# Feed-forward input with the tokens as rows: h2 stationary, 512 weight columns moving, products turned back

## The chip, the cores and the metric

The kernel runs on one NeuronCore of a Trainium2 chip. The metric is the device time of one execution in microseconds, as the median of several runs. All times below are of that core.

## The reference

One layer of a hybrid diffusion backbone (256 latent tokens, 256 context tokens, width 2048, float32): an adaLN-modulated mixer (multi-head latent attention and bidirectional HGRN2, merged by gates), then an adaLN-modulated SwiGLU feed-forward. Cut to what matters here:

```python
D_MODEL, SEQ, CTX_LEN = 2048, 256, 256
D_FF = 5632                      # 44 blocks of 128

def mixer_projections(h, w_in_l, ...):
    p = h @ w_in_l               # for the latent and for the context stream
    c_q, c_kv, k_r, hg_q, hg_ff, hg_fb, hg_i, hg_g, gate_logits = jnp.split(p, ...)
    ...
    hq = heads(jax.nn.silu(hg_q)) * (HG_FDIM ** -0.5)

def swiglu(h, w_in_l, w_out_l):
    a, b = jnp.split(h @ w_in_l, 2, axis=-1)
    return (jax.nn.silu(a) * b) @ w_out_l

# in reference(), last layer (the only one):
x = x + gt_a * rmsnorm(out_l, norm_g[layer, 1])
h = modulate(rmsnorm(x, norm_g[layer, 2]), sh_f, sc_f)          # h2 below
x = x + gt_f * rmsnorm(swiglu(h, w_ffn_in[layer], w_ffn_out[layer]), norm_g[layer, 3])
```

Of the context stream, only what the latent one needs is computed (keys, values, HGRN2 states). c_q, hg_q, hg_g and the gates are needed for the latent stream alone: these are the single-stream blocks.

## The kernel before

Every large product is made of three: a float32 value is split into a high part H (rounded to fp32r by ScalarE, a CAST) and a low part L (the difference, by VectorE), and weight times activation is H·H + H·L + L·H, added up in PSUM. Weights come as tiles `raw` of 128 x 2048 (1 MB) on SP's queue through three buffers (`load_w`), and are split in halves of 1024 columns into `wH` and `wL`, which have three buffers each (`split_w`). Activations live split in the tile `hx`, two parts side by side.

There are two ways to lay a product out.

- Weights stationary: a 128x128 block of the weight stands in TensorE and the 256 tokens move. `mm3` issues three matmuls (H with aH, H with aL, L with aH), of 256 columns for one stream or 512 for two. `mm_wide` has one stream's aH and aL side by side and issues H with both (512 columns) and L with aH (256); the two halves of the PSUM bank are then added by a ScalarE copy and a VectorE addition. The result has features as rows.
- Tokens as rows: `project_tok` makes 128 tokens of the activation stationary and moves 512 weight columns, for both token halves `hf`. It takes two PSUM banks (`ps`), and per k and half three matmuls of 512. The result has tokens as rows. The output projection (wout) and the feed-forward's output (wfo) use it.

The order of the work, with TensorE's part in each stage: the first modulation; latents and the first blocks of the input projection; eight HGRN heads (`hgrn_head`), in each of which two of the five blocks are single-stream ones with `mm3`; gates (`mm_wide`) woven into attention; branch merge (wbr); output projection (wout) with the norm behind it; then, from 992.6 us, the second norm and h2; feed-forward in three parts, input blocks (`ffn_in`) and after them that part's share of the output (`ffn_out`), which is added up in `y`; the last norm.

h2 is made so: `x1` (tokens as rows) is scaled by 1/rms per token (`scaled`, `rt2`), turned by TensorE (`pxt`, a 128x128 transpose per block and token half), and ScalarE applies A2 and SH2 (1 + scale times norm gain, and shift), now one value per row, and writes the high part; VectorE recomputes the value (`xm`) and subtracts. The first four feed-forward blocks (`ffn_first`) take h2 row block by row block as it comes, with `mm3`'s three matmuls of 256. The other 84 blocks are pairs (a and b of 128 features) in `ffn_in`, with `mm_wide`. `swish` makes silu(a)·b and splits it into `G`, already with features as rows, as the output wants it.

The second modulation's 64 weight rows are reduced on VectorE, one 2048-wide multiply-and-sum each (`mod_job`), spread through the stages; 16 of them fall into the feed-forward. They feed A2, SH2 and the gates `g1b` and `g2b`, which go through DRAM (`gdr`) to come back as rows on all partitions (`gate_rows`).

The program is recorded in the order of the code, and a scheduler then sets the order on each engine; `tc.issue_after(x)` holds what is issued under it back behind x. PSUM has four banks in pool `pj` (projections) and four in `px` (transposes, small products). Each engine runs its own list in order, and waits by semaphores for the others.

Of the kernel before, what the change touches and what calls it, by code (L numbers as in the profile page):

```python
# [7 lines left out]
F32 = mybir.dt.float32  # L8
# [18 lines left out]
def block_kernel(  # L27
# [15 lines left out]
    wfs: bass.AP,  # L43
# [125 lines left out]
    def both(k, e):  # L169

        return hx[:, :, k, e, :]
# [180 lines left out]
    def project(nb, streams):  # L352
        if nb < NPRE:
            return pre[nb]
        w = split_w(load_w(win[nb - NPRE]))
        ps = pj.tile([P, 512], F32, tag="pj", name="ps")
        for k in range(KD):
            if len(streams) == 2:
                o, act = ps.rearrange("p (s t) -> p s t", s=2), (both(k, 0), both(k, 1))
# [11 lines left out]
    def latent(blocks, streams, width, gains, dst, n, tags):  # L371
        ss = px.tile([P, 512], F32, tag="px", name="ss")
        raws = []
        for i, nb in enumerate(blocks):
            ps = project(nb, streams)
            r = wk.tile([P, width], F32, tag=tags[i], name=f"lat{i}")
            nc.scalar.copy(r, ps[:, 0:width])  # L377
# [62 lines left out]
    def hgrn_head(h):  # L440
# [126 lines left out]
        nc.scalar.activation(qs, psq[:, 0:T], AF.Sigmoid)  # L567
        nc.vector.scalar_tensor_tensor(qs, qs, 128.0 ** -0.5, psq[:, 0:T], op0=ALU.mult, op1=ALU.mult)
# [11 lines left out]
        nc.scalar.activation(sgg, psg[:, 0:T], AF.Sigmoid)  # L580
        nc.vector.scalar_tensor_tensor(sgg, sgg, ogt, psg[:, 0:T], op0=ALU.mult, op1=ALU.mult)
# [189 lines left out]
    gdr = dp.tile([2, KD, P], F32, name="gdr")  # L771

    def gate_rows(i, tiles):

        nc.vector.tensor_tensor(gts[:, i], mod2[:, 3 * i], b2[:, 2 + 3 * i], op=ALU.add)
        nc.vector.tensor_tensor(gts[:, i], gts[:, i], gsm[:, 1 + 2 * i], op=ALU.mult)
        pg = px.tile([P, 512], F32, tag="px", name="pg")
        nc.tensor.transpose(pg[0:KD, 0:P], gts[:, i], ident)
# [7 lines left out]
    def project_tok(tiles, nk, src, first, last, lead=None):  # L786
# [6 lines left out]
        for q in range(nq):  # L793
# [11 lines left out]
            with ExitStack() as es:  # L805
                for n_, (k, hf) in enumerate(order):
# [3 lines left out]
                    aH, aL = (src[k][:, e, hf * P:(hf + 1) * P] for e in range(2))  # L810
                    for n, (l, r) in enumerate(((aH, H), (aL, H), (aH, L))):
                        mm = nc.tensor.matmul(ps[hf], l, r, start=(k == 0 and n == 0), stop=(k == nk - 1 and n == 2))  # L812
        return ps
# [20 lines left out]
    for c in range(4):  # L834
        nc.sync.dma_start(xr[:, :, c * 512:(c + 1) * 512], xn[:, :, c * 512:(c + 1) * 512])
    r1 = []
    ssq = wk.tile([P, 32], F32, name="ssq")[:, 0:24].rearrange("p (i h c) -> p i h c", i=3, h=2)
    for c in range(4):
        cs = slice(c * 512, (c + 1) * 512)
        ps = project_tok(lambda q: wout[c, q], KD, mg, True, True,  # L840
# [9 lines left out]
    wfs0 = split_into(load_w(wfs[0]), pairs([wide(u) for u in spare[8:]]))  # L850
    xsc = [[None] * 4, [None] * 4]
# [9 lines left out]
    def scaled(hf, c, eng):  # L861
        xq = ap.tile([P, 512], F32, tag="hC", name="xq", bufs=8)
        x_ = x1[:, hf, c * 512:(c + 1) * 512]
        if eng is nc.scalar:
            nc.scalar.activation(xq, x_, AF.Identity, scale=rt2[hf])
        else:
            nc.vector.tensor_scalar(xq, x_, rt2[hf], None, op0=ALU.mult)
        xsc[hf][c] = xq

    scaled(0, 0, nc.vector)  # L870
    scaled(1, 0, nc.vector)
    h2 = []
    for c in range(4):
        for kp in range(2):
            pt = px.tile([P, 2, T], F32, tag="px", name="pxt")
            for hf in range(2):
                for i in range(2):
                    q = slice((2 * kp + i) * P, (2 * kp + i + 1) * P)
                    nc.tensor.matmul(pt[:, i, hf * P:(hf + 1) * P], xsc[hf][c][:, q], ident,
                                     is_transpose=True, start=(i + hf == 0), stop=(i + hf == 2))  # L880
            for i in range(2):
                j = 4 * c + 2 * kp + i
                h = units[j]
                hi = nc.scalar.activation(h[:, 0, :], pt[:, i], AF.Identity, bias=SH2[:, j:j + 1], scale=A2[:, j:j + 1])
                xm = wk.tile([P, T], F32, tag="hf", name="xm", bufs=2)
                nc.vector.tensor_scalar(xm, pt[:, i], A2[:, j:j + 1], SH2[:, j:j + 1], op0=ALU.mult, op1=ALU.add)
                lo = nc.vector.tensor_tensor(h[:, 1, :], xm, h[:, 0, :].bitcast(F32), op=ALU.subtract)
                h2.append((h, lo))
            if kp == 0 and c < 3:
                with tc.issue_after(lo.ins):  # L890
                    scaled(0, c + 1, nc.vector)
                with tc.issue_after(hi.ins):
                    scaled(1, c + 1, nc.scalar)
# [3 lines left out]
    n_g = [0]  # L897

    def ffn_first():

        pss = [pj.tile([P, 512], F32, tag="pj", name=f"psf{i}") for i in range(2)]
        for q in range(4):
            with tc.issue_after(h2[3 * q][1].ins):
                w = wfs0 if q == 0 else split_w(load_w(wfs[q]))
            for kk in range(4):
                k = 4 * q + kk
                for b in range(4):
                    H, L = w((kk * 4 + b) * P, P)
                    o = pss[b // 2][:, (b % 2) * T:(b % 2 + 1) * T]
                    for n, (l, r) in enumerate(((H, h2[k][0][:, 0, :]), (H, h2[k][0][:, 1, :]), (L, h2[k][0][:, 0, :]))):  # L910
                        nc.tensor.matmul(o, l, r, start=(b % 2 == 0 and k == 0 and n == 0),  # L911
                                         stop=(b % 2 == 1 and k == KD - 1 and n == 2))
        for j in range(2):
            swish(j, pss[j])

    def ffn_in(j):
        s_ = wk.tile([P, 512], F32, tag=("f", "kk")[j % 2], name="s_")
        for i in range(2):
            w = split_w(load_w(wfi[2 * (j - 2) + i]))
            ps = pj.tile([P, 512], F32, tag="pj", name="psf")  # L920
            for k in range(KD):
                mm_wide(ps, w(k * P, P), h2[k][0], k == 0, k == KD - 1)
            half = s_[:, i * T:(i + 1) * T]
            nc.scalar.copy(half, ps[:, 0:T])
            nc.vector.tensor_tensor(half, half, ps[:, T:2 * T], op=ALU.add)
        swish(j, s_)

    def swish(j, ps):
        sa = wk.tile([P, T], F32, tag="hf", name="sa", bufs=2)
        nc.scalar.activation(sa, ps[:, 0:T], AF.Silu)  # L930
        nc.vector.tensor_tensor(sa, sa, ps[:, T:2 * T], op=ALU.mult)
        part = j // 16
        slot_c = part == 1 and j < 24
        if slot_c:
            g = ap.tile([P, 2, T], F32R, tag="hC", name="hC", bufs=8)
        else:
            g = spare[n_g[0] % 16]
            n_g[0] += 1
        split_act(g, sa)
        G[j] = g  # L940
# [4 lines left out]
    def ffn_out(part):  # L945
        q0 = 4 * part
        nq = min(4, NFF // 4 - q0)
        for c in range(4):
            cs = slice(c * 512, (c + 1) * 512)
            ps = project_tok(lambda q: wfo[c, q0 + q], 4 * nq, G[4 * q0:], part == 0, part == 2,  # L950
                             pairs([ap.tile([P, 512], F32R, tag="hC", name="wl", bufs=8) for _ in range(8)])
                             if part == 2 and c == 3 else None)
# [17 lines left out]
    ffn_first()  # L970
    nxt = 2
    for part in range(3):
        upto = min(NFF, 16 * part + 18) if part < 2 else NFF
        while nxt < upto:
            ffn_in(nxt)
            nxt += 1
            mod_job(1)
# [3 lines left out]
        ffn_out(part)  # L981
# [13 lines left out]
_INS = ["xn", "xT", "ctxT", "small", "crep", "wm1", "wm2", "wst", "win", "wqk", "wv", "wbr", "wout", "wfs", "wfi",  # L995
# [3 lines left out]
def _layout(i):  # L999
# [62 lines left out]
    def quads(w):  # L1062

        k = w.shape[0] // 512
        return w.reshape(k, 4, P, 4, 512).transpose(3, 0, 2, 1, 4).reshape(4, k, P, 2048)
# [4 lines left out]
    c4 = np.concatenate([rng(0), rng(half), rng(P), rng(half + P)])  # L1070
    o["wfs"] = wi[:, c4].reshape(4, 4, P, 512).transpose(0, 2, 1, 3).reshape(4, P, 2048)
    o["wfi"] = blocks(wi, np.concatenate([np.concatenate([rng(j * P), rng(half + j * P)]) for j in range(2, NFF)]))
# [45 lines left out]
```

## Time and profile before

| | |
|---|---|
| median of 3 runs | 1753.96 us (1753.0 to 1754.22) |
| profiled execution | 1755.65 us, of which the span is 1753.8 us |
| TensorE busy | 97% of the span, granted clock 0.99 on average |
| VectorE, ScalarE busy | 63%, 45% |
| weight traffic | 382.87 MB, 218 GB/s on average |

TensorE's matmuls overlap: the duration of one is longer than its distance to the next, so rates are read from the length of a stage and the number of matmuls in it. PEld is the loading of the stationary operand, beside the matmuls. A view of stages gives length, busy time by engine with the number of instructions, and the clock that TensorE was granted.

### The profile page before, as it was taken

How to read it: one execution, taken by the hardware profiler on the slowest of the kernel's cores; microseconds unless marked ns; L12 is line 12 of the kernel's file. 1: busy time of each engine (PE TensorE's matmuls, PEld its weight loads, DVE VectorE, ACT ScalarE, POOL GpSimd, SP SyncE). 2: the span in 40 equal slices, each digit the busy share in tenths (PEclk: the TensorE clock that was granted, in tenths of full speed). 3: DMA queues.
4: the chain of work that ended last, by engine and by line, in shares of the span. 5: the costliest groups of instructions: out<-in, count | busy, mean ns of one | idle time of the engine just before them, and what ended most of it. 6: DMA issues, size and time to landing. Idle time of an engine off the chain costs nothing.

```text
span 1753.8 us, 24343 instructions
## 1 busy us (share of the span) xinstructions
PE 1707.0 (97%) x9714; PEld 1457.3 (83%) x9714; DVE 1113.2 (63%) x1702; ACT 780.7 (45%) x1162; POOL 56.2 (3%) x81
## 2 busy tenths in 40 slices
PE   6898999999999999999999899999999999999997
PEld 4457988888889888889998798888888888888886
DVE  5335777777668766666665687776445555555556
ACT  5225433333334444445544654444444444344443
POOL 0200000000000000001310000000000000000000
PEclk9999999999999999999999899999999999999999
DMA  9974355655556575588765367777555555555553
GB/s 381 364 296 174 145 192 192 214 195 192 176 184 230 191 252 187 191 304 294 272 240 192 146 216 286 287 274 258 194 191 189 192 185 182 195 192 184 192 192 120
DMA packets 59649, 382.87 MB, mean 218 GB/s; under 512 B 7024, under 2 KB 7824, under 8 KB 16272
## 3 DMA queue, kind: packets, MB, share of 16 engines
q1 hardware_dynamic: 54720, 367.09, 58.2%
q0 software_dynamic: 4096, 13.11, 2.0%
q8 instruction: 76, 1.25, 0.3%
q10 hardware_dynamic: 720, 1.12, 0.2%
q14 instruction: 37, 0.30, 0.0%
HBM read 374.99 MB, written 6.31 MB: 217 GB/s over the span
## 4 chain that ended last, share of the span: by engine, by line
PE 95%; DMA 2%; DVE 1%; ACT 1%; issue 0%; SPq 0%; DVEq 0%; ACTq 0%
PE ps L145 20%; PE pst L812 18%; PE psf L149 18%; PE psf L150 9%; PE ps L149 7%; PE psb L750 5%; PE pre L145 4%; PE ps L150 3%; DMA raw<-in_wm_dram 2%; PE psf L911 1%; PE pm L283 1%; PE psS L688 1%; PE po L712 1%; PE psS L685 1%; PE pv L660 1%; PE pq L644 1%
## 5 line engine op out<-in xcount | busy, mean ns | idle before, releaser
L111 DVE TENSOR_TENSOR wL<-raw,wH 128x1024 fp32r<-128x1024 f32 x480 | 587.4, 1226 | 451.3 <-ACT wH L109 449.4
L109 ACT CAST wH<-raw 128x1024 fp32r<-128x1024 f32 x480 | 501.9, 1047 | 728.4 <-PE ps L145 189.8
L149 PE MATMUL psf<-hx,wH 128*128 128x512 f32 x1344 | 475.2, 399 | 0.0
L150 PE MATMUL psf<-hx,wL 128*128 128x256 f32 x1344 | 377.5, 281 | 0.0
L145 PE MATMUL ps<-hx,wH 128*128 128x512 f32 (+1 forms) x1312 | 330.3, 341 | 1.3 <-ACT lat L377 1.3
L149 PEld LDWEIGHTS psf<-hx,wH 128*128 128x128 f32 x1344 | 252.6, 188 | 62.8
L150 PEld LDWEIGHTS psf<-hx,wL 128*128 128x128 f32 x1344 | 253.9, 189 | 0.3
L145 PEld LDWEIGHTS ps<-hx,wH 128*128 128x128 f32 x1312 | 226.1, 190 | 28.1 <-ACT lat L377 1.5
L812 PE MATMUL pst<-wH,hx 128*128 128x512 f32 x800 | 231.3, 389 | 0.0
L145 PE MATMUL ps<-hx,wL 128*128 128x512 f32 (+1 forms) x656 | 223.9, 341 | 1.2 <-DVE wL L111 1.2
L149 PE MATMUL ps<-hx,wH 128*128 128x512 f32 x512 | 184.1, 400 | 0.0
L812 PEld LDWEIGHTS pst<-wH,hx 128*128 128x128 f32 x800 | 150.0, 188 | 31.0
L347 DVE CUSTOM_DVE_ANT_0 raw<-raw,cb 128x2048 f32<-128x2048 f32 x64 | 146.1, 2283 | 35.8 <-DMA raw<-in_wm_dram 35.7
L150 PE MATMUL ps<-hx,wL 128*128 128x256 f32 x512 | 143.6, 281 | 0.0
L812 PE MATMUL pst<-wL,hx 128*128 128x512 f32 x400 | 140.5, 389 | 0.0
L145 PEld LDWEIGHTS ps<-hx,wL 128*128 128x128 f32 x656 | 124.4, 190 | 14.4 <-DVE wL L111 1.4
L149 PEld LDWEIGHTS ps<-hx,wH 128*128 128x128 f32 x512 | 96.1, 188 | 23.2 <-issue 1.7
L150 PEld LDWEIGHTS ps<-hx,wL 128*128 128x128 f32 x512 | 96.5, 189 | 2.4 <-DVE mx L690 1.1
L812 PEld LDWEIGHTS pst<-wL,hx 128*128 128x128 f32 x400 | 75.1, 188 | 15.8
L145 PE MATMUL pre<-hx,wH 128*128 128x512 f32 (+1 forms) x204 | 67.1, 412 | 5.3 <-ACT hx L202 5.2
L145 PEld LDWEIGHTS pre<-hx,wH 128*128 128x128 f32 x204 | 40.1, 208 | 26.7 <-ACT hx L202 10.4
L750 PE MATMUL psb<-hx,wH 128*128 128x256 f32 x256 | 46.8, 283 | 0.0
(427 smaller groups left out, 1741.9 us busy)
## 6 DMA issues: line engine op xcount, KB each, us to landing
raw<-in_wm_dram SPq DMA_DIRECT2D x96, 1024.0 KB, 4.9
raw<-in_wfi_dram SPq DMA_DIRECT2D x84, 1024.0 KB, 4.8
raw<-in_win_dram SPq DMA_DIRECT2D x73, 1024.0 KB, 4.9
raw<-in_wfo_dram SPq DMA_DIRECT2D x44, 1024.0 KB, 4.8
raw<-in_wbr_dram SPq DMA_DIRECT2D x16, 1024.0 KB, 5.1
raw<-in_wout_dram SPq DMA_DIRECT2D x16, 1024.0 KB, 4.8
raw<-in_wqk_dram SPq DMA_DIRECT2D x4, 1024.0 KB, 5.3
sgd<-sgx POOLq DMA_DIRECT2D x16, 256.0 KB, 5.9
```

What stands on the lines that cost most here:

```text
L109: nc.scalar.copy(H, raw[:, o:o + n])
L111: nc.vector.tensor_tensor(L, raw[:, o:o + n], H.bitcast(F32), op=ALU.subtract)
L145: nc.tensor.matmul(o, l, r, start=(first and i == 0), stop=(last and i == len(seq) - 1))
L149: nc.tensor.matmul(ps, w[0], act.rearrange("p e t -> p (e t)"), start=first, stop=False)
L150: nc.tensor.matmul(ps[:, 0:T], w[1], act[:, 0, :], start=False, stop=last)
L283: nc.tensor.matmul(pm[32 * (k % 4):32 * (k % 4) + 32, 0:n], cst[:, k], raw[:, kk * n:(kk + 1) * n], start=(k < 4), stop=(k >= KD - 4))
L347: nc.vector.tensor_tensor_reduce(out=raw, in0=raw, in1=cbt[0], scale=1.0, scalar=0.0, op0=ALU.mult, op1=ALU.add, accum_out=mod2[:, i // KD ...
L644: nc.tensor.matmul(pq[:, i * T:(i + 1) * T], l, r, start=(k == 0 and i == 0 and z == 0), stop=(k == 3 and i == 1 and z == 2))
L660: nc.tensor.matmul(pv[:, i, :], ckvs[:, k, l, ts_], r, start=(i == 0 and k == 0 and z == 0), stop=(i == 1 and k == 1 and z == 2))
L685: nc.tensor.matmul(psS, qn[a][:, i * T + qb * P:i * T + (qb + 1) * P], kn[b], start=(n == 0), stop=False)
L750: nc.tensor.matmul(ps[:, br * T:(br + 1) * T], l, r, start=(br == 0 and k == 0 and z == 0), stop=(br == 1 and k == NH - 1 and z == 2))
L812: mm = nc.tensor.matmul(ps[hf], l, r, start=(k == 0 and n == 0), stop=(k == nk - 1 and n == 2))
```

## The change

1. Feed-forward input: `ffn_in` now uses `project_tok`. Per group j of 512 features, two chunks (a, then b) of 512 weight columns each: 16 k x 2 halves x 3 = 96 matmuls of 512 columns, instead of 4 blocks of 16 pairs. Silu and product are done with tokens as rows (`sa`, `g_row`), and `turn` transposes the four blocks of `g_row` back for `G`; it is called by a hook behind the first quarter of the next chunk. `ffn_first` goes; `first_chunk` takes its place.
2. h2: A2 becomes a row on all partitions (`A2b`, by `rows`, through DRAM), so one VectorE instruction scales by 1/rms and A2 before the transpose. High and low parts are then written in pieces of 128x128, token half 0 first; 32 of each instead of 16.
3. `project`'s 20 single-stream blocks (four of c_q, two in each head) use `mm_wide`, and `joined` adds the two halves.

The same number of weight loads is made (84 + 4 before, 88 after), in another layout.

```diff
@@ project
-                o, act = ps[:, 0:T], (hx[:, 0, k, 0, :], hx[:, 0, k, 1, :])
-            mm3([o], w(k * P, P), [act], k == 0, k == KD - 1)
+                mm_wide(ps, w(k * P, P), hx[:, 0, k], k == 0, k == KD - 1)
+    def joined(ps, r):
+        nc.scalar.copy(r, ps[:, 0:T])
+        nc.vector.tensor_tensor(r, r, ps[:, T:2 * T], op=ALU.add)
+        return r
@@ hgrn_head (psq; the same for psg, and in latent)
-        nc.scalar.activation(qs, psq[:, 0:T], AF.Sigmoid)
+        qv = joined(psq, wk.tile([P, T], F32, tag="hf", name="qv", bufs=2))
+        nc.scalar.activation(qs, qv, AF.Sigmoid)
@@ project_tok
+            if q == 0 and hook:
+                hook()
@@ before the output projection
+    A2b = rows(2, A2, [wk.tile([P, 512], F32, tag=t, name="A2b") for t in ("kt", "ktn", "vT", "vn")])
@@ h2
+    for hf in range(2):
+        ts_ = slice(hf * P, (hf + 1) * P)
+        for c in range(4):
+            xq = ap.tile([P, 512], F32, tag="hC", name="xq", bufs=8)
+            nc.vector.scalar_tensor_tensor(xq, x1[:, hf, c * 512:(c + 1) * 512], rt2[hf], A2b[c], op0=ALU.mult, op1=ALU.mult)
+            pt = px.tile([P, 4, P], F32, tag="px", name="pxt")
+            for i in range(4):
+                nc.tensor.matmul(pt[:, i], xq[:, i * P:(i + 1) * P], ident, is_transpose=True, start=(i == 0), stop=(i == 3))
+            for i in range(4):
+                j = 4 * c + i
+                h = units[j]
+                hi = nc.scalar.activation(h[:, 0, ts_], pt[:, i], AF.Identity, bias=SH2[:, j:j + 1], scale=1.0)
+                lo = nc.vector.scalar_tensor_tensor(h[:, 1, ts_], pt[:, i], SH2[:, j:j + 1], h[:, 0, ts_].bitcast(F32),
+                                                    op0=ALU.add, op1=ALU.subtract)
+            h2[hf, c] = (hi, lo)
@@ first_chunk (in place of ffn_first): splits held behind h2's first tiles, then
+        products(range(0, 10), 0)
+        products(range(0, 10), 1)
...
+        for k in range(10, KD):
+            for hf in range(2):
+                products((k,), hf)
@@ ffn_in
+                ps = project_tok(lambda q: wfi[2 * j + i, q], KD, lambda k: units[k], True, True, None,
+                                 hook if i == 0 else None)
+            mod_job(1)
+            for hf in range(2):
+                if i == 0:
+                    sa.append(wk.tile([P, 512], F32, tag=("vT", "vn")[hf], name="sa"))
+                    nc.scalar.activation(sa[hf], ps[hf], AF.Silu)
+                else:
+                    g_row.append(wk.tile([P, 512], F32, tag=("kt", "ktn")[hf], name="g_row"))
+                    nc.vector.tensor_tensor(g_row[-1], ps[hf], sa[hf], op=ALU.mult)
+    def turn(j):
+        g = g_row[2 * j:]
+        for b in range(0, 4, 2):
+            pt = px.tile([P, 2, T], F32, tag="px", name="pgt")
+            for i in range(2):
+                for hf in range(2):
+                    nc.tensor.matmul(pt[:, i, hf * P:(hf + 1) * P], g[hf][:, (b + i) * P:(b + i + 1) * P], ident,
+                                     is_transpose=True, start=(i + hf == 0), stop=(i + hf == 2))
+            for i in range(2):
+                G[4 * j + b + i] = u = spare[(4 * j + b + i) % 16]
+                split_act(u, pt[:, i])
```

What the scheduler makes of it stands here at three places. First TensorE's list at the start of the feed-forward, before; `pst` on top is the end of the output projection, `pxt` are h2's transposes, `psf` the first four blocks:

```order
L812 MATMUL pst<-hx 128x512 x12
L879 MATMUL pxt<-c_82,xq 128x128 x8
L911 MATMUL psf_9002<-hx 128x256
L911 MATMUL psf_9003<-hx 128x256
L911 MATMUL psf_9002<-hx 128x256 x5
L911 MATMUL psf_9003<-hx 128x256 x5
```

The same place after (L919 is the first chunk's products):

```order
L825 MATMUL pst<-hx 128x512 x12
L884 MATMUL pxt<-c_82,xq 128x128 x8
L919 MATMUL pst<-hx 128x512
L884 MATMUL pxt<-c_82,xq 128x128 x8
L919 MATMUL pst<-hx 128x512 x9
L884 MATMUL pxt<-c_82,xq 128x128 x4
L919 MATMUL pst<-hx 128x512 x2
L919 MATMUL pst<-wH,hx 128x512 x2
```

Before, eight transposes (four blocks of both halves) opened the way to 48 matmuls; after, the sixteen transposes of half 0 stand among ten matmuls, and the tile behind those needs the first tile's PSUM bank again.

Second, VectorE's list at that place after the change, from the second norm's last reciprocals on (`xq` is the scaling, L871 the residual of token half 1, L889 a low part; the numbers behind rt and pxt tell the halves and tiles apart):

```order
L840 RECIPROCAL rt10_8606<-rt10_8606 128x1
L840 RECIPROCAL rt01_8579<-rt01_8579 128x1
L881 SCALAR_TENSOR_TENSOR xq_8626<-x1_7978,rt10_8606,A2b_7984 128x512
L881 SCALAR_TENSOR_TENSOR xq_8641<-x1_7978,rt10_8606,A2b_7985 128x512
L871 SCALAR_TENSOR_TENSOR x1_7978<-x1_7978,rt01_8579,xr_7979 128x512 x4
L881 SCALAR_TENSOR_TENSOR xq_8656<-x1_7978,rt10_8606,A2b_7986 128x512
L881 SCALAR_TENSOR_TENSOR xq_8671<-x1_7978,rt10_8606,A2b_7987 128x512
L889 SCALAR_TENSOR_TENSOR hx_87<-pxt_8628,SH2_7958,hx_87 128x128
```

Before, both halves' residuals came first, and then one scaling of each half:

```order
L825 RECIPROCAL rt_8834<-rt_8834 128x1
L856 SCALAR_TENSOR_TENSOR x_8246<-x_8246,rt_8834,xr 128x512 x2
L825 RECIPROCAL rt_8861<-rt_8861 128x1
L856 SCALAR_TENSOR_TENSOR x_8246<-x_8246,rt_8834,xr 128x512 x2
L867 TENSOR_SCALAR xq<-x_8246,rt_8861 128x512
```

Half 0's scaling has moved ahead of half 1's residual, half of it at least; its first low part stands behind all four scalings.

Third, VectorE's list in the steady part after the change, around the end of a b chunk (`raw_9294` is its last quarter, `raw_9337`, `raw_9389` and `raw_9423` the first three of the next chunk; ISA with `mod2` is a modulation job):

```order
L110 TENSOR_TENSOR wL_9302<-raw_9294,wH_9300 128x1024
L110 TENSOR_TENSOR wL_9341<-raw_9337,wH_9339 128x1024
L110 TENSOR_TENSOR wL_9345<-raw_9337,wH_9343 128x1024
L952 TENSOR_TENSOR g_row_9331<-pst_9190,sa_9186 128x512
L952 TENSOR_TENSOR g_row_9333<-pst_9191,sa_9188 128x512
L110 TENSOR_TENSOR wL_9393<-raw_9389,wH_9391 128x1024
L110 TENSOR_TENSOR wL_9397<-raw_9389,wH_9395 128x1024
L110 TENSOR_TENSOR wL_9427<-raw_9423,wH_9425 128x1024
L133 TENSOR_TENSOR hx_87<-pgt_9371,hx_87 128x256
L133 TENSOR_TENSOR hx_87<-pgt_9380,hx_87 128x256
L133 TENSOR_TENSOR hx_87<-pgt_9371,hx_87 128x256
L133 TENSOR_TENSOR hx_87<-pgt_9380,hx_87 128x256
```

and next

```order
L346 ISA raw_9491,mod2_1082<-raw_9491,cb_1323 128x2048
L346 ISA mod2_1082 128x1
L110 TENSOR_TENSOR wL_9431<-raw_9423,wH_9429 128x1024
L110 TENSOR_TENSOR wL_9461<-raw_9457,wH_9459 128x1024
L110 TENSOR_TENSOR wL_9465<-raw_9457,wH_9463 128x1024
```

The products `g_row` stand behind both halves of the next chunk's first quarter, and a modulation job stands ahead of the second half of its third.

More of the change, by code (lines that the diff above doesn't have):

```diff
@@ L859, in block_kernel @@
         rt2.append(rstd_part(1, hf))
[L861 to L875, printed above, removed]
-            for hf in range(2):
-                for i in range(2):
-                    q = slice((2 * kp + i) * P, (2 * kp + i + 1) * P)
-                    nc.tensor.matmul(pt[:, i, hf * P:(hf + 1) * P], xsc[hf][c][:, q], ident,
+    h2 = {}
@@ L896, in block_kernel @@
-    G = [None] * NFF
[L897 to L914, printed above, removed]
```

137 lines of the change are left out of this document (71 added, 66 removed).

## Prediction

> **What bounds the kernel now.** I read the page's engine totals first, then the chain that ended last, then the table of stages.
>
> ```profile
> span 1753.8 us, 24343 instructions
> PE 1707.0 (97%) x9714; PEld 1457.3 (83%) x9714; DVE 1113.2 (63%) x1702; ACT 780.7 (45%) x1162; POOL 56.2 (3%) x81
> PE 95%; DMA 2%; DVE 1%; ACT 1%; issue 0%; SPq 0%; DVEq 0%; ACTq 0%
> 191.00:540.00 349.00, 349.00 (x2013) 307.47 (x2012) 262.11 (x544) 130.50 (x174) 0.00 (x0) 1.00 0.55 191
> 992.60:1032.20 39.60, 33.37 (x243) 31.85 (x243) 32.89 (x60) 23.13 (x44) 0.00 (x0) 0.87 0.29 97
> 1210.07:1297.15 87.08, 87.08 (x386) 72.08 (x385) 40.28 (x35) 38.26 (x42) 0.00 (x0) 1.00 0.60 205
> 1297.15:1478.04 180.89, 180.89 (x1026) 156.79 (x1025) 100.06 (x125) 85.51 (x128) 0.00 (x0) 1.00 0.53 186
> 1565.14:1678.19 113.05, 113.05 (x642) 97.99 (x641) 62.84 (x79) 52.88 (x79) 0.00 (x0) 1.00 0.53 186
> ```
>
> The last five rows are stages: length, then busy time of PE, PEld, DVE, ACT and POOL, then the granted clock. TensorE has 95% of the chain, and in the HGRN heads (191 to 540), a feed-forward output part (1210 to 1297) and two feed-forward input parts (1297 to 1478, 1565 to 1678) it is never idle at full clock, while VectorE is busy for 46 to 75% of them. So what a change is worth there is TensorE's time for the new stream of matmuls, and vector and scalar work counts only where TensorE comes to wait for it. The one place with idle TensorE that the change touches is 992.6 to 1032.2: the second norm, h2 and the first four blocks. The profiled execution took 1755.65 us (1.85 around its span); I apply differences to the median of the runs, 1753.96.
>
> **Feed-forward input, the main term.** Busy time per matmul overlaps its neighbour, so I take stage length over count. The parts 1297 to 1478 and 1565 to 1678 are 32 and 20 blocks of 16 pairs (one matmul of 512 and one of 256 columns): 293.94 us / 832 = 353.3 ns a pair, 5.65 us a block. The new form is what the output parts run already, three matmuls of 512 per k and token half:
>
> ```profile
> 1210.07 87.08 PE pst L812 x384
> 1006.59 0.87 PE pxt L879 x8
> 1007.47 5.76 PE psf L911 x48
> 1001.87 4.72 PE psf L911 x24
> L704 PE MATMUL pp<-c,sgx 128*128 128x128 f32 x64 | 8.9, 272 | 0.0
> ```
>
> The first four are pieces of the chain (start, length, count). 87.08/384 = 226.8 ns. A chunk of 512 columns replaces four blocks: 96 x 226.8 = 21.77 against 22.61 us. The 84 blocks behind the first four become 21 chunks: 474.8 to 457.2, **-17.6 us**. The moving columns are equal (768 x 4 x 16 = 96 x 512); what goes is that the mixed pair costs 460 ns per 1000 columns and the uniform stream 443.
>
> The products must be turned back: 11 turns of eight 128x128 transposes. Eight such took 0.87 us between matmuls (109 ns each): 11 x 0.87 = **+9.6**. They stand behind the first quarter of the next chunk, 24 x 0.227 = 5.4 us after the product that they need has ended. VectorE reaches the two multiplications after one split that was waiting for the old chunk: some 0.9 + 2 x 0.7 = 2.3 us (durations below), so 3 us are left and TensorE should not wait.
>
> The Trainium skill (TensorE: Matmul & The Clock Gate, Back-to-back issue gap) gives columns/2.4 + 2.5 ns per matmul when isolated. By it a pair is 325 ns and a 512 matmul 215.8, so the main term would be -1.7 and not -17.6. The rows of this kernel are 353.3 and 226.8, and I go by them.
>
> **Wait that could come in the steady part.** With turns the splits of one quarter queue behind the four low halves of the turn and behind a modulation job, whose operand takes a weight buffer and is fetched only when that buffer's split is over.
>
> ```profile
> L111 DVE TENSOR_TENSOR wL<-raw,wH 128x1024 fp32r<-128x1024 f32 x480 | 587.4, 1226 | 451.3 <-ACT wH L109 449.4
> L347 DVE CUSTOM_DVE_ANT_0 raw<-raw,cb 128x2048 f32<-128x2048 f32 x64 | 146.1, 2283 | 35.8 <-DMA raw<-in_wm_dram 35.7
> raw<-in_wm_dram SPq DMA_DIRECT2D x96, 1024.0 KB, 4.9
> L753 DVE TENSOR_TENSOR sgx<-psb,sgx 128x512 f32<-128x512 f32 x16 | 10.9, 684 | 2.4 <-PE psb L750 2.4
> L134 DVE TENSOR_TENSOR hx<-sa,hx 128x256 fp32r<-128x256 f32 x36 | 15.1, 418 | 0.0
> ```
>
> Counted from a chunk's end: the buffer is free at 5.1, the fetch lands at 10.0, the job ends at 12.4, the split behind it at 13.6, and TensorE wants it at 14.5 (10.9 + 0.87 + 2.72). That is 0.9 us to spare, so I take 0 and an upper bound of 1 us in each of the eight chunks that have both. Otherwise a chunk has 8 splits, one job and 1.4 us of products, 13.5 us of VectorE in 21.8. The jobs come at half the density of before, and end with the second part. Weight traffic is equal (88 loads).
>
> **The beginning: h2 and the first chunk.** Before, the part ends at 1032.2, but 8 or 9 pairs of the next block were already done by then (rows below): worth 3.0, so it ends in effect at 1029.2.
>
> ```profile
> L149 PE MATMUL psf<-hx,wH 128*128 128x512 f32 x10 | 3.7, 398 | 0.0
> L150 PE MATMUL psf<-hx,wL 128*128 128x256 f32 x8 | 2.3, 282 | 0.0
> 997.60:1001.87 4.27, 3.03 (x10) 1.93 (x10) 1.78 (x5) 2.39 (x7) 0.00 (x0) 0.50 0.00 2
> 1001.87:1006.40 4.53, 4.53 (x24) 4.53 (x25) 4.38 (x9) 1.26 (x3) 0.00 (x0) 0.60 0.00 0
> 1006.40:1012.90 6.50, 6.50 (x57) 6.50 (x56) 5.82 (x11) 2.77 (x6) 0.00 (x0) 1.00 0.48 164
> L856 DVE SCALAR_TENSOR_TENSOR x<-x,rt,xr 128x512 f32<-128x512 f32 x8 | 5.5, 746 | 0.1
> L884 ACT ACTIVATE hx<-pxt,SH,A 128x256 fp32r<-128x256 f32 x16 | 8.6, 560 | 7.9 <-PE pxt L879 5.0 <-DVE xm L886 2.9
> L707 ACT COPY pT<-pp 128x128 f32<-128x128 f32 x32 | 7.5, 268 | 9.0 <-DVE pT L707 8.9
> L524 DVE TENSOR_SCALAR st<-pu,dec 128x128 f32<-128x128 f32 x16 | 5.5, 347 | 19.4 <-PE pu L521 19.4
> 994.04 0.15 DVE L823 TENSOR_REDUCE rt<-ssq 128x1 f32<-128x4 f32 x1
> ```
>
> The 16 scalings of 256 columns become 32 of 128, each with its low half behind it. A second piece of the same tile waited for VectorE (the 2.9 us of xm), so the pieces of a tile go one after another. Prices by the nearest rows: high piece between 0.27 and 0.56 us, I take 0.43; low piece 0.3, under the 0.35 of the row with a factor. In VectorE's new order half 0 is ready for scaling at about 994.5 (its reduction was done by 994.2). Before the low half of its fourth block stand 12 instructions of 512 columns, half 1's residual and scaling among them (about 0.72 each), and 9 of 128: 8.6 + 3.0 with itself, 1006.1, and with the waits on ScalarE's squares about 1007. TensorE stands there, because the fifth transposed tile reuses the first one's bank. From then 86 matmuls and 16 transposes remain, 19.5 + 1.7. The clock was 0.5 to 0.6 while the work trickled, and came back after some 4 us of dense work: the 24 matmuls of 256 in 4.72 us cost 1.8 more than 24 x 0.12. With 1.8 again the first chunk ends at 1030.0: **+0.8**. Ends of this term: TensorE fed from 997 on, 997 + 25.3 + 1.8 = 1024.1, -5; all pieces one after another (32 x 0.73 = 23.4 from 996), five splits and a job among them (8.4), and 14 last matmuls with the slow clock (5), 1033, +4; I keep +5. The saved 1.3 us of the four blocks' form (192 x 0.12 against 96 x 0.2268) are in it.
>
> **Single-stream blocks.** 20 blocks go from 48 matmuls of 256 to 16 pairs.
>
> ```profile
> 333.38 0.40 PE L145 MATMUL ps<-hx,wH 128*128 128x256 f32 x2
> 339.13 0.63 PE L145 MATMUL ps<-hx,wH 128*128 128x512 f32 x2
> L609 ACT COPY sgx<-ps 128x256 f32<-128x256 f32 x32 | 11.6, 366 | 0.0
> L610 DVE TENSOR_TENSOR sgx<-sgx,ps 128x256 f32<-128x256 f32 x32 | 13.1, 413 | 0.0
> 298.54 0.29 DVE L490 TENSOR_TENSOR kt<-kt,rdec 128x128 f32<-128x128 f32 x1
> 302.23 0.60 PE L498 MATMUL pk<-c,kt 128*128 128x128 f32 x4
> ```
>
> One block fills the time between the first two rows: 5.75 us, against 5.65 for 16 pairs. 20 x 0.10 = **-1.9** (unrounded). Joining adds 0.37 + 0.41 us off TensorE; VectorE in the heads goes from 75 to 77%. The chain behind it ends in keys that TensorE transposes; they were ready at 298.83 and taken at 302.23 (last two rows), so 3.4 us cover the 0.8. With that cover gone it would be 0.8 x 20 = 16 us; the zero idle time speaks against it, and I keep +2 as the end.
>
> **A2 as rows.**
>
> ```profile
> 904.92 28.03 SPq L101 DMA_DIRECT2D raw<-in_wout_dram  x6
> 921.71 1.05 ACT L109 CAST wH<-raw 128x1024 fp32r<-128x1024 f32 x1 [1.67 <-PE pst L812]
> raw<-in_wout_dram SPq DMA_DIRECT2D x16, 1024.0 KB, 4.8
> ```
>
> One transpose ahead of the output projection, 0.3 at most. On SP's queue its 8 KB write and four broadcasts stand between the fourth and the fifth weight load. The fifth went out at about 910.5 (six in 28.03 us), landed 4.8 later and was wanted at 921.71, so it has 6 us in hand against the 1 or 2 that the five small transfers hold the queue. **+0.3** (0 to 1). Output parts and end are untouched.
>
> Sum: -17.6 + 9.6 + 0.8 - 1.9 + 0.3 = -8.8, so 1753.96 - 8.8 = 1745.2.
>
> **Rivals.**
> - *h2 starves TensorE.* The first chunk ends near 1035 and the modulation jobs cost a few us more: -17.6 + 9.6 + 5 + 3 - 1.9 + 0.3 = -1.6, 1752.4. For it: two engines pass small pieces in turn. Against: 23 us of pieces lie beside 21 us of matmuls. 0.12.
> - *Slower: transposes that do not overlap.* If each turn costs eight whole durations, 272 ns each (row of pp) and not 109, 88 x 0.163 = +14.3 and the time is 1759.5. It decides from 0.21 us a transpose on. Against: the chain's 0.87 for eight at full clock. The Trainium skill (TensorE: Matmul & The Clock Gate, Part 4: PE-mode transpose) has about 275 ns in one kernel's context; by that figure the sum would be +5.8; the trace disagrees with 109. 0.05.
> - *Slower: the new form saves nothing per column.* With 460 ns per 1000 columns for the chunks too, the main term is 0: +8.8, 1762.8. By the Trainium skill's rule on the issue gap, above, the sum would be +7.1. Against: both rates stand in one trace at clock 1.00. 0.05.
> - *Better start.* TensorE fed from 997: -5 in place of +0.8, so -14.6, 1739.4. For it: half 0 no longer waits for half 1. 0.1.
>
> **Numbers.** The forecast itself has 0.68, with its own span of 1742 to 1749. The range 1739 to 1752 reaches to the better start and into the starved one. A measurement here tells about 0.2% (3.5 us) from no change: faster 0.79, same 0.11, slower 0.10.
>
> **What would show it.** Right: a chunk of the input part at 21.8 us and a turn at 0.9 in the chain, no idle TensorE from about 1030 to the end, the heads shorter by 1.5 to 2 us. Wrong: TensorE waiting for g_row, for wL behind a modulation job, or for h2's pieces past 1010; matmuls of the chunks further apart than 227 ns.

## The result: 1741.1 us, 13 us faster, and the profile after

The changed kernel took 1741.08 us (median of 4 runs, 1738.74 to 1742.93) against 1754.09 us for the kernel before (4 runs, 1753.0 to 1754.82). The ratio is 0.9926, 95% interval 0.9908 to 0.9943: between 10.0 and 16.1 us less. The forecast was 8.8 us less.

The profiled execution took 1740.55 us. Two lines of its page, the span and the engines' busy time:

```profile
span 1738.8 us, 22134 instructions
PE 1694.0 (97%) x8715; PEld 1410.4 (81%) x8715; DVE 1089.0 (63%) x1619; ACT 766.2 (44%) x1086; POOL 51.7 (3%) x81
```

TensorE has 999 matmuls fewer and is 13.0 us less busy, and it bounds the kernel as before. Where the time went is read from the table of stages (length; busy time of PE, PEld, DVE, ACT, POOL; granted clock; DMA share; GB/s). First the kernel after, from the start of the first latent block (c_q); the first row holds latents, heads and gates:

```profile
144.69:808.20 663.51, 660.73 (x3575) 562.57 (x3574) 483.21 (x891) 295.35 (x454) 11.91 (x22) 1.00 0.57 204
808.20:900.50 92.30, 92.30 (x773) 92.27 (x771) 69.25 (x73) 45.60 (x59) 19.96 (x25) 1.00 0.71 260
987.80:1001.20 13.40, 7.72 (x31) 6.04 (x32) 12.68 (x30) 9.55 (x29) 0.00 (x0) 0.75 0.00 1
1001.20:1022.15 20.95, 20.95 (x99) 17.31 (x99) 15.96 (x32) 14.09 (x29) 0.00 (x0) 1.00 0.55 201
1022.15:1728.50 706.35, 706.33 (x3162) 585.51 (x3160) 391.28 (x382) 304.32 (x348) 1.76 (x1) 1.00 0.59 211
```

The rows of the kernel before that answer to the first two and to the last (the last begins at 1029.2, where the first four blocks ended in effect):

```profile
148.39:813.10 664.71, 662.19 (x3895) 578.54 (x3894) 477.21 (x871) 287.83 (x438) 11.86 (x22) 1.00 0.57 203
813.10:905.40 92.30, 92.30 (x772) 92.29 (x771) 66.45 (x73) 44.23 (x59) 24.59 (x25) 1.00 0.73 264
1029.20:1743.57 714.37, 714.36 (x3752) 609.90 (x3751) 422.61 (x489) 329.46 (x456) 1.76 (x1) 1.00 0.59 210
```

Read row by row: latents, heads and gates 1.2 us shorter; the blend projections unchanged; from the output projection's end to the first chunk's end 34.35 us (13.40 + 20.95), where before it was 36.6; from there to the last product 8.0 us shorter. Beside these, the stage ahead of the latents ended 3.7 us earlier, though nothing in it was changed. -1.2 - 2.25 - 8.0 - 3.7 is the -15.1 between the two profiled executions (1755.65 and 1740.55).

The chain of the changed kernel in the feed-forward part (start, length, what, count) has the chunks and the turns:

```profile
1049.36 0.87 PE pgt L961 x8
1050.23 43.54 PE pst L825 x192
1093.77 0.88 PE pgt L961 x8
```

192 matmuls are the two chunks between two turns: 226.8 ns each, 21.77 us a chunk. Eight turned tiles take 0.87 us. No piece of another engine lies between them. All of TensorE's waits in the part that the change touches:

```profile
PE pxt L884 <- DVE xq L881: 4.8, 2, 2.4
PE ps L148 <- DVE lat L367: 2.8, 1, 2.8
PE pxt L884 <- DVE hx L889: 0.9, 1, 0.9
```

(Total us, times, longest.) Two are at the start of the feed-forward part, one at the latents; after 1001.2 TensorE waits for nothing until its last product.

### The profile page after: what moved, and what is told of

Same layout as the page of the kernel before. It is cut to its first block, busy times and chain, and to the rows that moved or that the text cites. A ratio compares the mean times of both kernels' runs of the same rounds, so it can differ in the third digit from the quotient of the medians.

```text
span 1738.8 us, 22134 instructions
## 1 busy us (share of the span) xinstructions
PE 1694.0 (97%) x8715; PEld 1410.4 (81%) x8715; DVE 1089.0 (63%) x1619; ACT 766.2 (44%) x1086; POOL 51.7 (3%) x81
## 4 chain that ended last, share of the span: by engine, by line
PE 94%; DMA 2%; DVE 2%; ACT 1%; issue 0%; SPq 0%; DVEq 0%; ACTq 0%
PE pst L825 45%; PE ps L144 13%; PE ps L148 11%; PE ps L149 5%; PE psb L760 5%; PE pre L144 3%; DMA raw<-in_wm_dram 2%; PE pm L282 1%; PE pst L919 1%; PE psS L698 1%; PE po L722 1%; PE psS L695 1%; PE pv L670 1%; PE pq L654 1%; PE pk L144 1%; PE pgt L961 1%
## 5 line engine op out<-in xcount | busy, mean ns | idle before, releaser
L825 PE MATMUL pst<-wH,hx 128*128 128x512 f32 x2272 | 660.6, 390 | 0.0
L825 PEld LDWEIGHTS pst<-wH,hx 128*128 128x128 f32 x2272 | 425.6, 188 | 87.7
L825 PE MATMUL pst<-wL,hx 128*128 128x512 f32 x1136 | 402.2, 389 | 0.0
L148 PE MATMUL ps<-hx,wH 128*128 128x512 f32 x832 | 300.6, 402 | 2.8 <-DVE lat L367 2.8
L825 PEld LDWEIGHTS pst<-wL,hx 128*128 128x128 f32 x1136 | 213.2, 188 | 44.4
L149 PE MATMUL ps<-hx,wL 128*128 128x256 f32 x832 | 235.6, 284 | 0.0
L144 PE MATMUL ps<-hx,wH 128*128 128x512 f32 x672 | 212.5, 395 | 0.0
L148 PEld LDWEIGHTS ps<-hx,wH 128*128 128x128 f32 x832 | 156.9, 189 | 40.2 <-DVE lat L367 3.1
L346 DVE CUSTOM_DVE_ANT_0 raw<-raw,cb 128x2048 f32<-128x2048 f32 x64 | 146.1, 2283 | 31.8 <-DMA raw<-in_wm_dram 31.6
L144 PEld LDWEIGHTS ps<-hx,wH 128*128 128x128 f32 x672 | 125.0, 188 | 25.2
L144 PE MATMUL ps<-hx,wL 128*128 128x512 f32 x336 | 131.7, 392 | 0.0
L144 PEld LDWEIGHTS ps<-hx,wL 128*128 128x128 f32 x336 | 63.1, 188 | 12.8
L760 PE MATMUL psb<-hC,wH 128*128 128x256 f32 x256 | 46.8, 283 | 0.0
L760 PEld LDWEIGHTS psb<-hx,wH 128*128 128x128 f32 x256 | 39.9, 192 | 0.0
```

The lines of the kernel that those rows point to most:

```text
L144: nc.tensor.matmul(o, l, r, start=(first and i == 0), stop=(last and i == len(seq) - 1))
L148: nc.tensor.matmul(ps, w[0], act.rearrange("p e t -> p (e t)"), start=first, stop=False)
L149: nc.tensor.matmul(ps[:, 0:T], w[1], act[:, 0, :], start=False, stop=last)
L346: nc.vector.tensor_tensor_reduce(out=raw, in0=raw, in1=cbt[0], scale=1.0, scalar=0.0, op0=ALU.mult, op1=ALU.add, accum_out=mod2[:, i // KD ...
L760: nc.tensor.matmul(ps[:, br * T:(br + 1) * T], l, r, start=(br == 0 and k == 0 and z == 0), stop=(br == 1 and k == NH - 1 and z == 2))
```

## The experiments

Seven kernels, in two sets; within a set all were compared with runs of the kernel before. This table stands for all of them. "First block" is where the first latent block starts (us), "heads" is from there to the first blend matmul (latents, heads and gates), "blend, out" from that to the start of the last matmul of the output projection (0.4 us ahead of its end), and "feed-forward" from there to the start of the last product. Savings against the kernel before go by the ratio; the difference of the medians can be an us or two away from it.

| kernel | median us | ratio to before, 95% | first block | heads | blend, out | feed-forward |
|---|---|---|---|---|---|---|
| before | 1754.09 | | 148.4 | 664.7 | 179.1 | 751.0 |
| after | 1741.08 | 0.9926 (0.9908-0.9943) | 144.7 | 663.5 | 179.2 | 740.7 |
| e1 feed-forward only | 1745.59 | 0.9947 (0.9934-0.9959) | 149.6 | 664.7 | 179.2 | 740.7 |
| e2 single-stream only | 1751.87 | 0.9985 (0.9976-0.9995) | 147.2 | 662.7 | 179.1 | 751.8 |
| e3 turns twice | 1750.52 | 0.9982 (0.9973-0.999) | 148.3 | 662.6 | 179.2 | 750.3 |
| e4 latents as before | 1742.5 | 0.9933 (0.9919-0.9946) | 145.3 | 662.8 | 179.2 | 740.6 |
| e5 before, sizes grouped | 1748.11 | 0.9965 (0.9951-0.9978) | 149.6 | 664.0 | 179.1 | 746.0 |
| e6 after, sizes grouped | 1740.51 | 0.9921 (0.9906-0.9936) | 146.1 | 660.8 | 181.1 | 740.6 |
| e7 half 0 held | 1741.17 | 0.9925 (0.9911-0.9939) | 146.1 | 662.1 | 179.2 | 741.2 |

The kernel before took 1754.14 us beside e1 to e4 and 1755.67 beside e5 to e7.

### e1 and e2: each half of the change alone

e1 is the changed kernel with the 20 single-stream blocks put back:

```diff
             else:
-                mm_wide(ps, w(k * P, P), hx[:, 0, k], k == 0, k == KD - 1)
+                o, act = ps[:, 0:T], (hx[:, 0, k, 0, :], hx[:, 0, k, 1, :])
+            mm3([o], w(k * P, P), [act], k == 0, k == KD - 1)
...
-                joined(ps, r)
+            nc.scalar.copy(r, ps[:, 0:width])
```

> The feed-forward input, its turns and the new h2 as in the changed kernel; the 20 single-stream blocks with three matmuls of 256 as before. Theory (by the stages of the two traces: feed-forward -8.0, its start -2.2, heads and latents -0.8): this kernel keeps about 10 of the gain and is 0.8 us slower than the changed one, some 1743 where the kernel before is 1754. Rival, the prediction's step: the single-stream blocks carry 1.9 us, so 1743 to 1744 and the heads alone 1.9 longer. On the first 145 to 149 us, which were 3.9 us shorter in the changed kernel's profile though no instruction there differs: if the new layout of the weight inputs does it, this kernel has it too (near 144.7 us to the first projected block in the profile, as long in every run); if it is chance, this stage scatters by some us from profile to profile.

e2 is the opposite: the kernel before with only the mixed blocks and `joined`, its feed-forward part untouched.

> The kernel before with the single-stream blocks as pairs of 512 and 256 and the two halves joined; the feed-forward and its inputs as before. Theory: 16 blocks in the heads give 16 x 0.11 = -1.8 us, the four latent blocks lose about 1 us because a PSUM bank is now given back by VectorE's addition and no longer by ScalarE's copy: -0.8 us in all, ratio 0.9995. Rival, the prediction's step: -1.9 us with the joining hidden everywhere, ratio 0.9989. If the shorter first stage comes with the inputs' layout, it is absent here.

Measured: e1 saves 9.3 us (7.2 to 11.6), e2 2.6 us (0.9 to 4.2). The halves add up to 11.9, and the whole gave 13.0 (10.0 to 16.1). By stages, e1 has the whole -10.3 in the feed-forward part and 0 in the heads; e2 has -2.0 in the heads and nothing in the feed-forward part (+0.8). The heads stages of the changed kernel and of e2, e3, e4 and e7, which have the mixed form in the heads, are 1.2 to 2.6 us shorter than before. The repeat from head to head shows it without scatter; in each kernel's chain one piece recurs once a head, before and after:

```profile
272.94 22.38 PE ps L145 x121
322.61 22.38 PE ps L145 x121
```

```profile
269.46 10.93 PE ps L144 x48
318.91 10.93 PE ps L144 x48
```

A head took 49.67 us and takes 49.45: 0.22 for its two blocks, 0.11 each (forecast 0.10).

e1 also ended a theory of mine, that the new program's layout lets the stage ahead of the latents end earlier: e1 has that layout and its first block came at 149.6. e3 is the changed kernel up to the first turn and had its first block at 148.3 us, the changed kernel at 144.7. That stage scatters from one profiled execution to the next; in the nine profiles of the table it ended between 144.7 and 149.6. Why is not shown: TensorE's waits for weights there are 3.7 us in e1 and 6.1 in e3, the other way round than the two ends.

### e3: is a turn really 0.87 us, and hidden behind nothing?

The transposes of each turn are issued twice into the same bank; the result is the same.

```diff
-            for i in range(2):
+            for i in (0, 1, 0, 1):
```

> The changed kernel with every transpose of the turns issued twice into the same place (the second overwrites the first): 88 transposes more, nothing else. Theory: eight cost 0.87 us and nothing waits, so +9.6 us, ratio to the changed kernel 1.0055. Rival: a transpose costs its whole duration of 272 ns, +24 us. Second rival: they fit into slack, 0.

Measured: 9.4 us slower than the changed kernel by the medians, 9.6 in the feed-forward stage. Its chain:

```profile
1052.01 1.75 PE pgt L961 x16
1053.76 43.54 PE pst L825 x192
```

Sixteen take 1.75 us where eight took 0.87, and the chunks keep their 43.54. So a turn stands on the path with all of its time, 109 ns a transpose, and nothing waits because of it. 88 x 0.109 is 9.6. The rival of 272 ns each is out. So is the Trainium skill's figure in its place here (TensorE: Matmul & The Clock Gate, Part 4: PE-mode transpose, about 275 ns in one kernel's context): that is near the busy time of one transpose (272 here), and the spacing in a run of eight is 109.

### e4: the new wait at the latents

The changed kernel has one wait of 2.8 us that before did not have under that name. e4 gives the four latent blocks their old form and keeps the mixed form in the heads.

```diff
+            elif 6 <= nb < 10:
+                mm3([ps[:, 0:T]], w(k * P, P), [(hx[:, 0, k, 0, :], hx[:, 0, k, 1, :])], k == 0, k == KD - 1)
...
-                joined(ps, r)
+            nc.scalar.copy(r, ps[:, 0:width])
```

> The changed kernel with the four latent blocks back at three matmuls of 256 and a plain copy; the heads stay mixed. Theory: TensorE's wait of 2.8 us for VectorE's addition in the latents goes, the four blocks lose 4 x 0.1 us: about -1 to -2 us against the changed kernel. Rival: the wait has its cause in the weight splits on VectorE and only gets another name: +0.4 us.

Measured: 1742.5, no gain. TensorE's waits at that place in e4:

```profile
PE ps L144 <- ACT lat L384: 1.3, 1, 1.3
PE ps L144 <- DVE wL L110: 1.2, 1, 1.2
```

The 2.8 us in one wait became 1.3 and 1.2 in two, as before. From the first latent block to the recurring piece of the heads e4 takes 124.0 us (145.29 to 269.32); with the join it is 124.8 in the changed kernel and 123.3 in e3 and e7. So a cost of the join cannot be seen in these profiles, and my theory of 1 us is not borne out.

### e5 and e6: what in the stream of pairs was slow?

The main term went by two measured rates, without a reason for them. Uniform streams give 226.8 ns for 512 columns and 119.8 for 256 (5.75 us for 48); together 346.6, but an alternating pair takes 353.3. e5 takes the kernel before and only groups the sizes, in the 84 feed-forward blocks and the 32 gate blocks; it has no turns, and the same number of matmuls.

```diff
-    def mm_wide(ps, w, act, first, last):
+    def mm_block(ps, w, act):
...
+        for g in range(0, KD, 8):
+            for k in range(g, g + 8):
+                nc.tensor.matmul(ps, w(k * P, P)[0], act(k).rearrange("p e t -> p (e t)"), start=(k == 0), stop=False)
+            for k in range(g, g + 8):
+                nc.tensor.matmul(ps[:, 0:T], w(k * P, P)[1], act(k)[:, 0, :], start=False, stop=(k == KD - 1))
```

> The kernel before with one change: in its 84 feed-forward input blocks and its 32 gate blocks, the sixteen pairs of a 512-column and a 256-column matmul are issued as eight of 512, then eight of 256, for each half of a weight tile, with the same operands. Theory 'alternating': a part of the cost is the change of size from one matmul to the next, so a block falls from 5.65 us towards 8 x 2 x (0.2268 + 0.1198) = 5.55 us (0.2268 from the output parts, 0.1198 from the single-stream blocks of 256 columns): the second and third input parts together from 293.9 to 288.4, the whole kernel 116 x 0.107 = 12.4 us faster than before, near 1741.7, about the time of the changed kernel without a single turn. Rival 'each matmul has its own rate whatever stands beside it': 353.3 ns a pair stays, 0 +- 3 us, near 1754.

Measured: 6.1 us faster than before (3.9 to 8.6; 7.6 by the medians), about half of the 12.4. The second and third input parts in e5, then its chain:

```profile
1296.10:1475.00 178.90, 178.90 (x1026) 157.46 (x1025) 100.12 (x125) 86.43 (x128) 0.00 (x0) 1.00 0.53 189
1562.10:1673.80 111.70, 111.70 (x641) 98.32 (x641) 62.85 (x78) 53.66 (x79) 0.00 (x0) 1.00 0.53 189
```

```profile
1052.63 1.84 PE psf L151 x8
1054.47 0.95 PE psf L153 x8
1055.42 1.84 PE psf L151 x8
```

The parts fell from 293.9 to 290.6 us. A group of eight pairs takes 1.84 + 0.95 = 2.79 us (1055.42 - 1052.63): 349.1 ns a pair, against 353.3 alternating and 346.6 if each size kept its uniform rate. So changing the size does cost time, 6.7 ns a pair when it happens in every pair, and grouping by eight gets 4.2 of it back. With an equal cost at each change, two changes in eight pairs in place of sixteen would leave 0.8 ns a pair and not 2.5; what the rest is was not followed. The part of the PSUM bank that is written changes with the size, and the two were not told apart. In the heads stage with the gates e5 is 0.7 us shorter, where 32 blocks would give 2.1; that stage varies by 1.4 us among the kernels with the same blocks in it (662.1 to 663.5), so this says little. The rival of a rate that each matmul has whatever stands beside it is refuted.

This splits the main term. Of its 17.6 us, 84 x 16 x 6.7 ns = 9.0 us is the alternation that the chunks no longer have. The other 8.6 us is that matmuls of 256 are dearer per column than those of 512 even in streams of their own (119.8 against 226.8/2 = 113.4 ns). With a straight line through these two sizes, all that the kernel has, a matmul takes (226.8 - 119.8)/256 = 0.418 ns a column and 12.8 ns by itself, and 21 chunks have 2016 matmuls where 84 blocks had 2688: 672 x 12.8 = 8.6. The Trainium skill's rule (TensorE: Matmul & The Clock Gate, Back-to-back issue gap: columns/2.4 + 2.5 ns for isolated matmuls) has the slope that is seen here, 0.417; the part per matmul is 12.8 in this kernel, not 2.5.

e6 is the changed kernel with the same grouping in the pairs that it still has, the gates and the single-stream blocks.

> The changed kernel with the same grouping in what it still runs as alternating pairs: 32 gate blocks and 20 single-stream blocks. Theory 'alternating': 52 x 0.107 = 5.5 us less than the changed kernel, near 1735.5; the gate stage 3.4 us shorter, the heads 2.1 us. Rival 'own rate': no change, near 1741. A smaller effect in the heads than in the gates would say that something beside TensorE limits the heads.

Measured: 1740.51, the same as the changed kernel within the scatter, where 52 x 16 x 4.2 ns = 3.5 us would follow from e5. The heads do repeat faster, every 49.34 us for 49.45 (3.4 ns a pair), and the stage of heads and gates shrank to 660.8, but the blend stage behind it grew from 92.3 to 94.2:

```profile
806.90:901.10 94.20, 92.84 (x773) 92.35 (x771) 65.72 (x74) 43.58 (x59) 24.94 (x25) 1.00 0.73 265
```

TensorE waited there, and so did ScalarE ahead of it (rows of e6: two of TensorE's waits, then three pieces of ScalarE's timeline with the idle time before them):

```profile
PE psb L762 <- ACT wH L108: 0.7, 1, 0.7
PE psb L762 <- DVE wL L110: 0.6, 1, 0.6
```

```profile
823.41 0.63 ACT L764 ACTIVATE sgx<-sgx 128x512 f32<-128x512 f32 x1 [4.14 <-DMA sgx<-sgd]
823.95 1.03 ACT L108 CAST wH<-raw 128x1024 fp32r<-128x1024 f32 x1
...
825.79 1.03 ACT L108 CAST wH<-raw 128x1024 fp32r<-128x1024 f32 x1
```

ScalarE stood 4.14 us for the gates that come back from DRAM, with the split of a weight queued behind. In the changed kernel the same place has 1.16:

```profile
819.12 0.63 ACT L762 ACTIVATE sgx<-sgx 128x512 f32<-128x512 f32 x1 [1.16 <-DMA sgx<-sgd]
```

In the other eight profiles no single wait there is above 2.8 us (e1), and TensorE has none behind it. So in e6's one profile most of what the grouped blocks saved became a wait for the gates' way through DRAM. That a shorter gate stage must do this was not separated from the scatter of the transfers.

### e7: did half 0 going ahead make the start faster?

VectorE scales token half 0 before half 1's residual in the changed kernel; e7 holds it back, with the same instructions.

```diff
+            with tc.issue_after(last_x.ins):
+                nc.vector.scalar_tensor_tensor(xq, x1[:, hf, c * 512:(c + 1) * 512], rt2[hf], A2b[c], op0=ALU.mult,
+                                               op1=ALU.mult)
```

> The changed kernel with the scaling of token half 0 held on VectorE until half 1's residual is written, as the kernel before had it; same instructions. Theory 'half 0 ahead': the 2.3 us gained between the output projection's end and the first chunk's end come from half 0 starting early, so that stretch grows from 34.4 us to 36 to 37.5 (half 1's residual is four pieces of about 0.72 us), time 1743 to 1744.5. Rival 'clock': the gain comes from the nine 512-column matmuls that bring the clock back early, and the pieces catch up: 34.4 +- 0.5, no change in time. Second rival: later pieces also bring the clock back later, 38 to 40 us, near 1745 to 1747.

Measured: 1741.17, and 741.2 us in the feed-forward stage against 740.7: no change that a run can show. The first transposed tile of half 0 starts 2.6 us later (992.80 for 990.21), and yet the trickle lasts as long. The stages of e7, to be laid beside 13.40 and 20.95 above:

```profile
987.60:1001.17 13.57, 6.82 (x32) 5.50 (x32) 12.37 (x30) 8.77 (x27) 0.00 (x0) 0.87 0.00 1
1001.17:1022.34 21.17, 21.17 (x99) 17.26 (x99) 16.41 (x32) 15.02 (x31) 0.00 (x0) 1.00 0.54 199
```

In both kernels VectorE is busy nearly throughout the trickle (12.68 of 13.40 us, 12.37 of 13.57): by these figures the sum of its work ends it, and these two orders of it make no difference. In the kernel before VectorE was not the bound. Five us of its trickle, and the end of its chain there:

```profile
997.00:1002.00 5.00, 3.15 (x11) 2.06 (x11) 2.35 (x8) 3.09 (x9) 0.00 (x0) 0.50 0.00 2
```

```profile
997.47 0.73 ACT junk L858 x2
...
998.42 0.30 ACT rt L824
...
998.94 0.50 DVE xq L867
```

There all scaling waited for ScalarE's squares of half 1, and VectorE was busy for 2.35 us of 5.

What, then, gave the 2.25 us? Not a shorter trickle. TensorE's last wait ended 9.25 us behind the output projection before (1001.87) and ends 12.74 behind it after (1000.54), 3.5 later; what remains behind it fell from 27.3 us to 21.6, 5.7 less. Of the 5.7, 1.8 is the slow clock, which before was still there for the 24 matmuls behind the wait; 1.3 is the form, 96 matmuls of 512 in place of 192 of 256; and the rest is matmuls and transposes that had run inside the longer trickle. So the form and the clock make up the gain, and the longer trickle gave back about 0.9. That it was the new order that brought the clock back earlier is not shown.

e7 does not decide for or against the rival 'clock': that foretold 34.4 +- 0.5 us, and 34.7 came. But its clock was slow for half as long as in the changed kernel, and its trickle lasted no less. The same five us in the changed kernel, and then in e7, with a granted clock of 0.59 and 0.90:

```profile
995.00:1000.00 5.00, 4.64 (x15) 3.53 (x13) 4.87 (x15) 3.66 (x11) 0.00 (x0) 0.59 0.00 2
```

```profile
995.00:1000.00 5.00, 3.45 (x16) 2.56 (x16) 4.83 (x14) 2.90 (x11) 0.00 (x0) 0.90 0.01 2
```

## Why the prediction was right, and where a term was off

The direction, the size and the mechanism were as forecast; the median lies in the range, 4.1 us below the forecast and 0.9 below the span of 1742 to 1749 that the forecast gave itself.

- *Main term, -17.6, and turns, +9.6.* They hold to the tenth: from the first chunk's end to the last product 706.35 us was measured, and 21 x 21.77 + 11 x 0.87 + the output parts (239.5) are 706.3. The reason behind the two rates was missing; e5 gives it.
- *Wait in the steady part, 0 with a bound of 1 us in eight chunks.* 0: no wait of TensorE after 1001.2.
- *The beginning, +0.8.* This is the term that was mis-sized: -2.25 (the same within 0.5 us in e1, e3, e4, e7). The chain of the changed kernel shows where TensorE stood for the last time:

```profile
999.97 0.53 DVE hx L889 x2
1000.49 0.04 issue
1000.54 0.66 PE pxt L884 x4
1001.20 2.31 PE pst L919 x10
```

  It got the late low half at 1000.54, 12.7 us behind the output projection's end at 987.80, where "about 1007" was 14.4 behind it (1007 - 992.6): 1.7 of the difference. The 0.9 us put down for waits on ScalarE's squares did not come, since VectorE was busy for 12.68 of those 13.40 us; the pieces were priced well (0.37 and 0.35 us, forecast 0.43 and 0.3). Of the other 0.8, 0.3 is the start (half 0's scaling began 1.6 us behind the output projection, not 1.9), and 0.5 is VectorE's 21 instructions, which the chain has at 11.1 us for 11.6. From 1000.54 the rest took 21.6 us, where 21.2 + 1.8 were put down: the other 1.4. The 1.8 for a slow clock was not paid, because the clock was back at 1.00 by then; ten of the 512-column matmuls had already run inside the trickle. The case "fed from 997 on" (-5) did not come either: TensorE had 7.72 us of work in 13.40, because VectorE was the bound.
- *Single-stream blocks, -1.9.* -1.2 to -2.6 by stages, 0.11 a block by the heads' repeat; the joining is hidden as argued. At the latents one wait of 2.8 us stands in place of two of 1.3 and 1.2 (e4).
- *A2 as rows, +0.3.* The blend and output stages are 179.1 and 179.2: 0.1 at most. That part was luck. The queue was not held for 1 or 2 us: the write went out at 901.76 and the next weight load only at 910.43, 8.7 us later, since the broadcasts waited for the write to land; that load took 6.9 us to land and not 4.8. The 6 us in hand were used up. A wait of SP's queue, and the split of that weight on ScalarE, which stands 0.6 us behind the even beat of the splits before it (2.72 us):

```profile
SPq L796 <- DMA gdr<-grow: 6.3, 1, 6.3
```

```profile
917.43 1.05 ACT L108 CAST wH<-raw 128x1024 fp32r<-128x1024 f32 x1 [2.21 <-DMA raw<-in_wout_dram]
```

  TensorE still had no wait there.
- *Rivals.* A starved start did not come; transposes of 272 ns are refuted by e3, and no saving per column by e1 and by the chunks' 226.8 ns a matmul. The better start came only in part: its forecast was -5, by feeding TensorE from 997 on, and TensorE was not fed so.

With the measured start the sum is -17.6 + 9.6 - 2.25 - 2.0 = -12.2 (-2.0 is the mean of the heads stage in the changed kernel, e2, e3, e4 and e7). The remaining 0.8 to -13.0 is inside the interval, and less than the scatter of the stage ahead of the latents.

## What to carry to other kernels

Cost a stream of matmuls by stage length over count, apart for each mixture of sizes: the same columns cost 443 ns per 1000 in uniform matmuls of 512, 455 in groups of eight and 460 alternating with 256. When an operand is prepared in a trickle, add up the work of the engine that is busy through it; which half went first moved nothing here. Look at what is left to do when the trickle ends, and at which clock: that, and not its length, made this start shorter. Where a small transfer waits for another on the queue of the weights, count the landing of the first in the time that the queue is held (here 8.7 us for five small transfers). A few us saved ahead of a transfer that the next stage waits for may only lengthen that wait; one profile shows it.

## What was not expected of the hardware

- An alternation of 512 and 256 columns costs 6.7 ns a pair more than the two sizes in streams of their own, at full clock and with TensorE never idle; grouped by eight it costs 2.5.
- A matmul has 12.8 ns of its own beside 0.418 ns a column, if its time is a straight line between 256 and 512 columns.
- The clock fell to 0.50 behind the output projection and came back to 1.00. In windows of 0.1 us it was low for 10.24 us in all three kernels with the old start (before, e2, e5), for 6.83 in the changed kernel, e1, e3, e4 and e6, and for 3.41 in e7: three, two and one times 3.41. In the changed kernel that was from 992.2 to 999.1, inside the trickle; before it was from 995.3 to 1005.5, 3.6 us beyond TensorE's last wait. In e7 it was back at 996.1, when one matmul of 512 columns and up to sixteen transposes had started. What in the trickle decides it was not tested.
- The stage ahead of the latents ended anywhere from 144.7 to 149.6 us in nine profiles; the changed kernel and e3, which are alike up to there, were 3.6 us apart.
